# Two groups of an MLP go together block by block, and the indexer's first half moves into the MLP's tail

## The chip, the cores and the metric

The kernel runs on one core of a Trainium2 chip. The metric is the device time of one execution in microseconds (us), as the median of repeated runs. A profile is one further execution, seen by the hardware profiler.

The engines are named as in the profile: PE is the matrix engine, DVE the vector engine, ACT the scalar engine, POOL the GpSimd engine, and SP the engine that issues most DMA transfers. SBUF is the on-chip memory, PSUM the accumulators that PE writes.

## The reference

Four residual layers on 512 tokens of width 1024, in single precision: a mixer of stick-breaking attention and a state-space model, an MLP, a mixer of sparse attention ("DSA"), an MLP. Each is followed by a layer norm.

```python
x = layer_norm(ALPHA * x + h, ln_mix_g[i], ln_mix_b[i])
x = layer_norm(ALPHA * x + sq_relu_mlp(x, mlp_w1[i], mlp_w2[i]), ln_ffn_g[i], ln_ffn_b[i])

def sq_relu_mlp(x, w1, w2):
    return jnp.square(jax.nn.relu(x @ w1)) @ w2          # D_FF = 4096
```

The sparse attention lets a small "indexer" choose for each query the 128 keys that it attends to:

```python
# mixer_dsa: qi has 8 heads of 32, ki one head of 32, wi 8 weights
rel = jax.nn.relu(jnp.einsum('bqhd,bsd->bqsh', qi_b, ki))
score = jnp.einsum('bqsh,bqh->bqs', rel, wi_b) * idx_scale
score = jnp.where(causal, score, -jnp.inf)
_, idx = lax.top_k(score, topk)                          # topk = 128
```

The first 128 queries (block 0) have at most 128 keys, so nothing is chosen for them.

## The kernel before, in words

Tokens are cut in four blocks of 128. The residual stream `x` is in SBUF with tokens on partitions; its transpose is kept as two halves, `xhi` and `xlo`, whose sum is the single-precision value, and a product is made of three matmuls (hi by hi, hi by lo, lo by hi: `mm3` at L129, and L380 to L382). Weights come raw by DMA (L101); ACT rounds them to `whi` (L104), and DVE or POOL subtracts to get `wlo` (L105).

The order of instructions on each engine is not written by hand. A scheduler under the kernel's language orders each engine's queue when the program is built, from the order in which the code asks for the operations and from its own estimate of when each is ready. The queue is then fixed: an instruction that waits holds up all that stand behind it on its engine.

**The first MLP** (`mlp`, L205). Hidden units are cut in eight groups of 512. Groups 0 to 5 go through three passes with fewer products (`down_chunk`). Groups 6 and 7 are done plainly: `up_split` gives their hidden units as halves, and `mlp_block` (L371) multiplies one block of 128 tokens by 512 output columns in PSUM and adds that to `x` (L387). Before the change, the first half of the columns of group 6 is done for all four blocks. Then, block by block, `both` does group 7's first half of the columns and groups 6 and 7 together in the second half, with the norm of a block (`layer_norm`, L172) following the blocks. A norm is a chain over DVE (L181 to L183), POOL (L184), DVE (L185, L189), eight PE transposes (L199), and a split by ACT (L202) and DVE (L203) into `xhi` and `xlo`. Its parameters `gb` are loaded at L168.

**The indexer** (`index_scores`, L1009) belongs to the next mixer. For two halves of the tokens, c=0 (tokens 0 to 255) and c=1 (256 to 511), it projects key and weights (64 columns of weights, `psi`) and twice 128 query columns (72 matmuls), splits the results into halves (`split`, L854 and L855), writes them to DRAM (`kd`, `qd`) and reads them back in another layout (`kist`, `qist`; L1053 to L1062). `score_block` (L1070) then does a query block: eight matmuls (`psx`, L1078), eight relus on ACT (L1080) and eight weighted sums on DVE (L1081). Blocks 1, 2 and 3 have 256, 384 and 512 keys. `top_keys` (L1106) finds the 128 best of each query on DVE: 16 steps of a MAX (eight maxima, L1113) and a MATCH_REPLACE (L1114), for block 1 first and then for blocks 2 and 3 in turn. `dist` (L1119) marks the keys that were chosen, and the attention (`sparse_attention`, L1121) needs it at L1143, the first step behind its logits (`psl`, L1136).

Besides, the mixer projects V (L1101 to L1103), K and Q (`psa`, L131 to L133), which fill PE while DVE works on the top-k.

Of the kernel before, what the change touches and what calls it, by code (L numbers as in the profile page):

```python
# [11 lines left out]
ALU = mybir.AluOpType  # L12
# [23 lines left out]
class Trunk:  # L36
# [59 lines left out]
    def weights(self, srcs, n=1024, eng=None, pool=None, parts=1, tag=None):  # L96

        nc = self.nc
        raw, hi, lo = self.w_tiles(pool, tag)
# [8 lines left out]
    def w_cols(self, w, c0, eng=None, pool=None, tag=None):  # L108
# [4 lines left out]
        hi, lo = self.weights(srcs, eng=eng, pool=pool, tag=tag)  # L113
        return hi.rearrange("p (k c) -> p k c", c=P), lo.rearrange("p (k c) -> p k c", c=P)
# [90 lines left out]
    def mlp(self, w1, w2, g, b, last):  # L205
# [7 lines left out]
        with self.tc.tile_pool(name=self.nm("mlp"), bufs=2, side="right", reuse_waits="tile") as hp:  # L213
# [17 lines left out]
            def up_split(grp):  # L231
                hhi, hlo = h_tile(F32R), h_tile(F32R)
                for f in range(4):
                    ps = self.proj_fm(w1, grp * 512 + f * P, None)
                    h = hp.tile([P, S], F32, tag="r", bufs=1, name=self.nm("r"))
# [5 lines left out]

            for hs in up_raw(0, True):
                pass
            u = hp.tile([P, 2, 512], F32, tag="u", bufs=1, name=self.nm("u"))
# [8 lines left out]
            ng = 8  # L253
            for grp, h in ((6, got[3]), (7, got[7])):
                ws = [[self.w_rows(w2, grp * 512 + i * 256, half * 512, pool=hp if half or grp < ng - 1 else self.wp,
                                   tag=(("b12", "b11")[half] if grp < ng - 1 else "b21") if half or grp < ng - 1
                                   else None)
                       for i in range(2)] for half in range(2)]
                part = lambda half, h=h, ws=ws: (*h, ws[half])
                if grp == ng - 2:  # L260
                    for t in range(NB):
                        self.mlp_block([part(0)], t, 0, False)
                    held = part(1)
                else:
                    def both(t):
                        self.mlp_block([part(0)], t, 0, False)
                        n = 256 if last and t == NB - 1 else 512
                        for c0 in range(0, 512, n):
                            self.mlp_block([held, part(1)], t, 1, False, c0, n)
                    self.blocks_and_norms([lambda t=t: both(t) for t in range(NB)], self.ln_params(g, b), last,  # L270
                                          2 if last else 1)
# [683 lines left out]
    def mixer_dsa(self, w_in, w_out, g, b):  # L955
        nc, tc = self.nc, self.tc
        act, vec, pool = nc.scalar, nc.vector, nc.gpsimd
        with tc.tile_pool(name="m1", bufs=1, reuse_waits="tile") as mp, \
                tc.tile_pool(name="m1d", bufs=1, space=DRAM) as dp, \
# [6 lines left out]
            for h in range(16):  # L966
                pool.memset(sc[64 * (h % 2):64 * (h % 2) + 64, h // 2:h // 2 + 1], -0.125 / slope(h))
            with tc.tile_pool(name="idxs", bufs=1, side="right", reuse_waits="tile") as sp:
                accs, drm = self.index_scores(w_in, ip, sp, dp)
# [39 lines left out]
    def index_scores(self, w_in, op, ip, dp):  # L1009
# [3 lines left out]
        drm = op.tile([P, S], F32, name="drm")  # L1013
        cm = op.tile([P, S], F32, name="cm")
# [3 lines left out]
        pool.memset(cm, 0.0)  # L1018
        pool.affine_select(out=cm, in_=cm, pattern=[[-1, S]], compare_op=ALU.is_ge, fill=LOW,
                           base=S - P, channel_multiplier=1)  # L1020


        raw, hi, lo = self.w_tiles()
# [8 lines left out]
        wk = [t[:, 0:n].rearrange("p (k c) -> p k c", c=64) for t in (hi, lo)]  # L1032
        wts = [wk] + [self.w_cols(w_in, 1536 + i * P) for i in range(2)]
        wi = op.tile([P, NB, 8], F32, name="wi")

# [166 lines left out]
```

## Time and profile before

| | |
|---|---|
| median of 3 runs | 1167.16 us (1166.71 to 1168.52) |
| the profiled execution | 1165.24 us |
| its span, first to last instruction | 1163.5 us |
| granted PE clock over the span | 0.988 |
| busy: PE, DVE, ACT, POOL | 1108.7, 841.5, 532.4, 173.1 us |

Times in the views are microseconds from the start of the span. A timeline row has start, duration, engine, line, operation, `out<-in`, shape and count; in brackets stands the idle time ahead of it and what ended it. A row of waits has engine, what was waited with, `<-` what it waited for, total, times, longest. A row of the windows has a stretch, its length, the busy time of PE, PE's weight loads, DVE, ACT and POOL with their numbers of instructions, then the granted PE clock (1.00 is full), the share of time in which DMA was busy, and GB/s. A row of the chain has start, duration and what the end waited on. A group's row ends with the total, the mean in ns and the idle time ahead of it. Matmuls overlap: their duration is longer than their spacing, and costs here go by the spacing.

### The profile page before, as it was taken

To read this page: it belongs to the slowest core of one execution; us is meant where nothing else is said; L and a number is where in the kernel's file an instruction comes from. 1 tells how busy PE (TensorE), PEld (TensorE's weight loads), DVE (VectorE), ACT (ScalarE), POOL (GpSimd) and SP (SyncE) were. 2 spreads that over 40 slices of the span, in tenths; PEclk is the share of its full clock that TensorE was granted. 3 is DMA by queue.
4 is the path that set the end of the run, shared out by engine and by line. 5 is a ranking of instruction groups with operands and counts; after the bars stand their busy time and mean duration, and the time that the engine had idled before them with its cause. 6 is when DMAs were issued, how large, how long until landed. Compare 5 with 4: busy or idle time off the path is not lost.

```text
span 1163.5 us, 15569 instructions
## 1 busy us (share of the span) xinstructions
PE 1108.7 (95%) x5860; PEld 923.6 (79%) x5860; DVE 841.5 (72%) x1255; ACT 532.4 (46%) x832; POOL 173.1 (15%) x201
## 2 busy tenths in 40 slices
PE   7988998999999999999999959998999999999997
PEld 6877876788888888888888847776988888888886
DVE  7997598694666866975668997538548668587736
ACT  5534387324444544554135427642445445445510
POOL 1043230320000000000021744325000000000001
PEclk9999999999999999999999989999999999999999
DMA  7526683751242242333056850025304414415101
GB/s 244 142 64 156 188 220 100 211 151 37 72 145 91 75 150 66 110 108 79 1 141 160 217 164 1 19 69 186 109 19 127 129 35 145 127 38 162 37 1 73
DMA packets 147307, 126.99 MB, mean 109 GB/s; under 512 B 24353, under 2 KB 115297, under 8 KB 147233
## 3 DMA queue, kind: packets, MB, share of 16 engines
q1 hardware_dynamic: 145552, 123.59, 36.7%
q10 hardware_dynamic: 1680, 2.41, 0.6%
q8 instruction: 46, 0.75, 0.3%
q14 instruction: 29, 0.23, 0.1%
HBM read 105.80 MB, written 5.37 MB: 96 GB/s over the span
## 4 chain that ended last, share of the span: by engine, by line
PE 80%; DVE 12%; DMA 3%; issue 2%; ACT 2%; SPq 1%; POOLq 0%; DVEq 0%; ACTq 0%
PE psa L133 11%; PE psa L132 11%; PE psa L131 11%; PE psb L313 7%; PE psb L311 7%; PE psb L312 7%; PE pso L949 3%; PE psb L382 3%; PE psb L381 3%; PE psb L380 2%; PE pst L942 2%; DVE acc L1114 2%; DVE top L1113 2%; PE psb L841 2%; PE psb L842 2%
## 5 line engine op out<-in xcount | busy, mean ns | idle before, releaser
L133 PE MATMUL psa<-xhi,wlo 128*128 128x512 f32 (+1 forms) x720 | 267.1, 372 | 0.0
L132 PE MATMUL psa<-xlo,whi 128*128 128x512 f32 (+1 forms) x720 | 266.6, 371 | 0.0
L131 PE MATMUL psa<-xhi,whi 128*128 128x512 f32 (+1 forms) x720 | 265.6, 371 | 0.2 <-ACT xhi L202 0.2
L104 ACT CAST whi<-raw 128x1024 fp32r<-128x1024 f32 (+1 forms) x129 | 133.3, 1046 | 200.9 <-PE psa L132 130.1
L105 DVE TENSOR_TENSOR wlo<-raw,whi 128x1024 fp32r<-128x1024 f32 (+1 forms) x102 | 127.8, 1258 | 80.5 <-ACT whi L104 79.7
L132 PEld LDWEIGHTS psa<-xlo,whi 128*128 128x128 f32 x720 | 135.7, 188 | 23.4 <-DVE xlo L203 0.4
L133 PEld LDWEIGHTS psa<-xhi,wlo 128*128 128x128 f32 x720 | 135.8, 189 | 23.1
L131 PEld LDWEIGHTS psa<-xhi,whi 128*128 128x128 f32 x720 | 135.0, 188 | 23.1 <-ACT xhi L202 0.5
L299 DVE TENSOR_TENSOR wlo<-b,whi 128x1024 fp32r<-128x1024 f32 x84 | 102.5, 1221 | 43.0 <-ACT whi L298 42.8
L311 PE MATMUL psb<-whi,whi 128*128 128x512 f32 x336 | 130.7, 389 | 0.0
L312 PE MATMUL psb<-wlo,whi 128*128 128x512 f32 x336 | 130.7, 389 | 0.0
L313 PE MATMUL psb<-whi,wlo 128*128 128x512 f32 x336 | 129.7, 389 | 0.0
L298 ACT CAST whi<-b 128x1024 fp32r<-128x1024 f32 x84 | 88.3, 1051 | 42.0 <-PE psb L313 30.2
L105 POOL TENSOR_TENSOR wlo<-raw,whi 128x1024 fp32r<-128x1024 f32 x27 | 70.8, 2632 | 132.5 <-ACT whi L104 131.4
L184 POOL TENSOR_TENSOR rs<-rs,two 128x1 f32<-128x1 f32 x16 | 22.7, 1417 | 423.8 <-DVE rs L183 423.8
L312 PEld LDWEIGHTS psb<-wlo,whi 128*128 128x128 f32 x336 | 63.1, 188 | 13.2
L313 PEld LDWEIGHTS psb<-whi,wlo 128*128 128x128 f32 x336 | 63.1, 188 | 13.1
L311 PEld LDWEIGHTS psb<-whi,whi 128*128 128x128 f32 x336 | 63.1, 188 | 13.0
L293 DVE TENSOR_TENSOR b<-b,b 128x1024 f32<-128x1024 f32 x48 | 63.1, 1320 | 11.4 <-DMA b<-in_w_dram 10.9
L298 ACT CAST whi<-h 128x1024 fp32r<-128x1024 f32 x36 | 38.0, 1054 | 54.0 <-PE psb L312 34.0
L299 DVE TENSOR_TENSOR wlo<-h,whi 128x1024 fp32r<-128x1024 f32 x36 | 43.9, 1220 | 14.0 <-ACT whi L298 13.5
L841 PE MATMUL psb<-whi,xhi 128*128 128x512 f32 x128 | 51.5, 410 | 0.8 <-DVE x L848 0.6
(263 smaller groups left out, 1955.4 us busy)
## 6 DMA issues: line engine op xcount, KB each, us to landing
raw<-in_w_dram SPq DMA_DIRECT2D x80, 512.0 KB, 4.1
b<-in_w_dram SPq DMA_DIRECT2D x48, 512.0 KB, 4.5
raw<-in_w_in_dram SPq DMA_DIRECT2D x29, 512.0 KB, 4.5
raw<-in_w_out_dram SPq DMA_DIRECT2D x16, 512.0 KB, 4.8
qst<-hl SPq DMA_DIRECT2D x48, 128.0 KB, 3.5
kst<-hl SPq DMA_DIRECT2D x24, 256.0 KB, 4.7
gb<-in_ln_g_dram SPq DMA_DIRECT2D x4, 512.0 KB, 4.1
gb<-in_ln_b_dram SPq DMA_DIRECT2D x4, 512.0 KB, 5.0
```

Source lines behind the costliest of these rows:

```text
L104: nc.scalar.copy(hi[:, c], raw[:, c])
L105: (eng or nc.vector).tensor_tensor(lo[:, c], raw[:, c], hi[:, c].bitcast(F32), ALU.subtract)
L131: mm(ps, lhi, rhi, start=start, stop=False)
L132: mm(ps, lhi, rlo, start=False, stop=False)
L133: mm(ps, llo, rhi, start=False, stop=stop)
L293: vec.tensor_tensor(o, p, q, op)
L298: act.copy(hi, src)
L299: vec.tensor_tensor(lo, src, hi.bitcast(F32), ALU.subtract)
L311: mm(ps, lh, bhi[:, k, :], start=i + k == 0, stop=False)
L312: mm(ps, lh, blo[:, k, :], start=False, stop=False)
L313: mm(ps, ll, bhi[:, k, :], start=False, stop=i + k == 2)
L841: nc.tensor.matmul(ps, chi[:, k, tok], whi, start=i == 0, stop=False)
```

## The change

- In the first MLP, groups 6 and 7 are multiplied together for both halves of the columns: 24 matmuls in one accumulation, twice per block. The pass of group 6 alone is gone there, and with it four of the twelve evacuations. The second MLP keeps it.
- The order of the tail is written out: blocks 0 and 1, norm 0, block 2, norm 1, the first part of the indexer, block 3, norm 2, norm 3, the second part of the indexer.
- The indexer's first part is c=0: keys and weights of tokens 0 to 255, the queries of tokens 128 to 255 alone (block 0 needs none; 128 columns per matmul in place of 256), the way through DRAM, and the scores of block 1. The second part is c=1, up to the way through DRAM; its scores and all top-k steps stay in the mixer.
- The buffers that this needs (`drm`, `kist`, `wi`, `acc1`) live from before the first MLP, the weight and split buffers of the indexer lie in the MLP's pools, the buffers `u` and `r` of the MLP share the tile of the norm's parameters, and the causal mask `cm` becomes a DVE operation at the start of each score block.

```diff
-            u = hp.tile([P, 2, 512], F32, tag="u", bufs=1, name=self.nm("u"))
+            ur = self.cp.tile([P, 2, D], F32, tag="gb", bufs=1, name=self.nm("ur"))
+            u, r = (ur[:, i, :].rearrange("p (h c) -> p h c", c=512) for i in range(2))
...
-            for grp, h in ((6, got[3]), (7, got[7])):
...
+            parts = lambda half: [(*got[3], w6[half]), (*got[7], w7[half])]
+            if last:
+                for t in range(NB):
+                    self.mlp_block([(*got[3], w6[0])], t, 0, False)
...
+            def both(t):
+                self.mlp_block(parts(0)[last:], t, 0, False)
+                n = 256 if last and t == NB - 1 else 512
+                for c0 in range(0, 512, n):
+                    self.mlp_block(parts(1), t, 1, False, c0, n)
+            gb = self.ln_params(g, b)
...
+                both(0)
+                both(1)
+                norm(0)
+                both(2)
+                norm(1)
+                e = early(hp)
+                next(e)
+                both(3)
+                norm(2)
+                norm(3)
+                next(e)
...
+            hls = hp.tile([P, 2, 2, 256], F32R, tag="b11", bufs=2, name=self.nm("hls"))
...
+                n = P if i and c == 0 else 256
+                at = slice(tok.stop - n, tok.stop)
...
-                hl = self.hl_tile()[:, :, 0:256]
+                hl = hls[:, i % 2, :, 0:n]
...
+            if c == 0:
+                qst = hp.tile([P, 1024], F32R, tag="b11", bufs=2, name="qist1")[0:96].rearrange(
+                    "p (h t) -> p h t", t=P)
+                self.load_index_queries(qst, P)
+                slots = itertools.count()
+                self.score_block(1, qst, self.acc1, lambda: rel[:, next(slots) % 4, :])
+            yield
...
-            nc.vector.scalar_tensor_tensor(acc, r, wi[:, qb, h:h + 1], acc if h else cm[:, S - nk:],
-                                           ALU.mult, ALU.add)
+        nc.vector.tensor_scalar(acc, self.drm[:, S - nk:], BIG, LOW, ALU.is_ge, ALU.mult)
+            nc.vector.scalar_tensor_tensor(acc, r, self.wi[:, qb, h:h + 1], acc, ALU.mult, ALU.add)
```

How this moves the queues, at three places. A number behind a name is that of the tile or weight. In the changed kernel the lines of `mlp_block` are L392 to L394 and L399, `psx` is L1114, the score sums are L1117, the splits of the indexer L867, and MAX and MATCH_REPLACE L1147 and L1148.

PE before, from the last matmul of the first MLP (L382, block 3) to the first of c=1 (`psi_5119`); `pst` are the transposes of norms 2 and 3:

```order
L382 MATMUL psb_4878<-whi_4688,h_4359 128x512
L131 MATMUL psi_5019<-xhi,whi_4995 64x256
...
L199 MATMUL pst_4914<-ident,x 128x128 x4
...
L131 MATMUL psi_5050<-xhi,whi_5003 128x256
...
L131 MATMUL psi_5079<-xhi,whi_5009 128x256
...
L199 MATMUL pst_4938<-ident,x 128x128 x4
...
L1065 MATMUL psw_5113<-ident,wiT_5048 128x8 x2
L131 MATMUL psi_5119<-xhi,whi_4995 64x256
```

PE in the changed kernel, from the end of norm 1's transposes to the first of c=1 (`psi_5105`); block 3 is `psb_5001` and `psb_5027`:

```order
L199 MATMUL pst_4838<-ident,x 128x128 x3
L131 MATMUL psi_4873<-xhi,wx_4850 64x256 [waits Activation_49]
...
L133 MATMUL psi_4930<-xhi,wx_4865 128x128
...
L392 MATMUL psb_5001<-whi_4591,h_4034 128x512
...
L1114 MATMUL psx_4969<-kist,qist_4964 128x256 [waits DMAHW6_49,DMAHW5_49,DMAHW7_49,DMAHW3_49,DMAHW2_49]
...
L393 MATMUL psb_5027<-wlo_4628,h_4363 128x512
...
L199 MATMUL pst_5063<-ident,x 128x128 x4
...
L1114 MATMUL psx_4985<-kist,qist_4964 128x256 [waits Activation_49]
...
L199 MATMUL pst_5087<-ident,x 128x128 [waits DVE_49]
...
L131 MATMUL psi_5105<-xhi,wx_4850 64x256 [waits Activation_49]
```

The 72 matmuls of c=0 went from behind block 3 to ahead of it, and four `psx` of block 1, which wait for DRAM, stand ahead of its last eight matmuls. Between block 3 and c=1 only the transposes of norms 2 and 3 and four `psx` are left.

DVE before, from the evacuation of block 3 (L387 with `psb_4878`) to the end of its norm (L189):

```order
L387 TENSOR_TENSOR x<-x,psb_4878 128x512
L181 BN_STATS st_4928<-x 128x6
L182 BN_AGGR mv_4929<-st_4928 128x2
L183 TENSOR_SCALAR rs_4930<-mv_4929 128x1
L185 SCALAR_TENSOR_TENSOR x<-x,mv_4929,gb_4693 128x1024
L203 TENSOR_TENSOR xlo<-pst_4914,xhi 128x4x128
L203 TENSOR_TENSOR xlo<-pst_4921,xhi 128x4x128
L189 SCALAR_TENSOR_TENSOR x<-x,rs_4930,gb_4693 128x1024
```

DVE in the changed kernel, the same stretch (L399 with `psb_5027`):

```order
L399 TENSOR_TENSOR x<-x,psb_5027 128x512
L1117 SCALAR_TENSOR_TENSOR acc_2456<-rel_4872,wi,acc_2456 128x256
L105 TENSOR_TENSOR wlo_5484<-raw_5482,whi_5483 128x1024
L181 BN_STATS st_5077<-x 128x6
L105 TENSOR_TENSOR wlo_5524<-raw_5522,whi_5523 128x1024
L203 TENSOR_TENSOR xlo<-pst_5063,xhi 128x4x128
...
L182 BN_AGGR mv_5078<-st_5077 128x2
...
L183 TENSOR_SCALAR rs_5079<-mv_5078 128x1
L185 SCALAR_TENSOR_TENSOR x<-x,mv_5078,gb_4638 128x1024
L1117 SCALAR_TENSOR_TENSOR acc_2456<-rel_4872,wi,acc_2456 128x256
L189 SCALAR_TENSOR_TENSOR x<-x,rs_5079,gb_4638 128x1024
```

Two weight splits and four score sums of block 1 came in between (two of the sums are at the places left out).

DVE before, from the last split of c=1 (`psi_5179`) to the first sum of block 2 (`acc_5258`):

```order
L855 TENSOR_TENSOR hl_5204<-psi_5179,hl_5204 128x256
L1081 SCALAR_TENSOR_TENSOR acc_5217<-rel_5225,wi,acc_5217 128x256
...
L1113 MAX top_5342<-acc_5217 128x8
L1114 MATCH_REPLACE acc_5217<-top_5342,acc_5217 128x256
...
L1113 MAX top_5357<-acc_5217 128x8
L1081 SCALAR_TENSOR_TENSOR acc_5258<-rel_5261,wi,cm 128x384
```

DVE in the changed kernel, the same stretch (`psi_5162` to `acc_5223`):

```order
L867 TENSOR_TENSOR hls_5103<-psi_5162,hls_5103 128x256
L1111 TENSOR_SCALAR acc_5223<-drm 128x384
...
L1147 MAX top_5316<-acc_2456 128x8
L1148 MATCH_REPLACE acc_2456<-top_5316,acc_2456 128x256
...
L1147 MAX top_5331<-acc_2456 128x8
L1117 SCALAR_TENSOR_TENSOR acc_5223<-rel_5235,wi,acc_5223 128x384
```

The sums of block 1 left this stretch. The top-k steps of block 1 (`acc_2456` is `acc1`) stand where they stood: behind the last split of c=1, five and a half of them ahead of the first sum of block 2.

More of the change, by code (lines that the diff above doesn't have):

```diff
@@ L94, in w_tiles, with weights @@
                 wp.tile([P, 1024], F32R, tag="wlo", bufs=4, name=self.nm("wlo")))
-    def weights(self, srcs, n=1024, eng=None, pool=None, parts=1, tag=None):
+    def weights(self, srcs, n=1024, eng=None, pool=None, parts=1, tag=None, tiles=None):
         nc = self.nc
-        raw, hi, lo = self.w_tiles(pool, tag)
+        raw, hi, lo = tiles or self.w_tiles(pool, tag)
         for view, src in srcs(raw):
@@ L234, in up_split @@
                     ps = self.proj_fm(w1, grp * 512 + f * P, None)
-                    h = hp.tile([P, S], F32, tag="r", bufs=1, name=self.nm("r"))
+                    h = r[:, f % 2, :]
                     nc.scalar.activation(h, ps, AF.Relu)
@@ L252, in mlp @@
                 hs = got[-1]
-            ng = 8
-            for grp, h in ((6, got[3]), (7, got[7])):
[L255 to L271, printed above, removed]
+            rows = lambda grp, half, **kw: [self.w_rows(w2, grp * 512 + i * 256, half * 512, **kw) for i in range(2)]
@@ new lines, in mlp @@
+            w6 = [rows(6, half, pool=hp, tag=("b12", "b11")[half]) for half in range(2)]
+            parts = lambda half: [(*got[3], w6[half]), (*got[7], w7[half])]
+            if last:
+                for t in range(NB):
+                    self.mlp_block([(*got[3], w6[0])], t, 0, False)
+            w7 = [rows(7, half, **(dict(pool=hp, tag="b21") if half and last else {})) for half in range(2)]
+            def both(t):
[3 more added lines that the diff above has]
+                    self.mlp_block(parts(1), t, 1, False, c0, n)
@@ new lines, in mlp @@
+            gb = self.ln_params(g, b)
+            if last:
+                self.blocks_and_norms([lambda t=t: both(t) for t in range(NB)], gb, last)
+            else:
+                norm = lambda t: self.layer_norm(t, gb, last)
+                both(0)
[9 more added lines that the diff above has]
+                next(e)
@@ L967, in mixer_dsa @@
                 pool.memset(sc[64 * (h % 2):64 * (h % 2) + 64, h // 2:h // 2 + 1], -0.125 / slope(h))
+            accs = [None, self.acc1] + [ip.tile([P, S], F32, tag="acc", bufs=2, name=self.nm("acc"))[:, :(qb + 1) * P]
+                                        for qb in (2, 3)]
+            drm = self.drm
             with tc.tile_pool(name="idxs", bufs=1, side="right", reuse_waits="tile") as sp:
-                accs, drm = self.index_scores(w_in, ip, sp, dp)
+                qst = sp.tile([96, 8, 256], F32R, name="qist")
+                self.load_index_queries(qst, 256)
+                for qb in (2, 3):
+                    rel = lambda: sp.tile([P, S], F32, tag="rel", bufs=4, name=self.nm("rel"))
+                    self.score_block(qb, qst[:, :, (qb - 2) * P:(qb - 1) * P], accs[qb], rel)
             vec.tensor_copy(dist[:, 0, 0:P], drm[:, S - P:])
@@ L1017, in index_scores, with tiles @@
                            base=S - P, channel_multiplier=1)
[L1018 to L1023, printed above, removed]
+        def tiles(tag):
+            raw = self.wp.tile([P, 1024], F32, tag="raw", bufs=3, name=self.nm("raw"))
+            return raw, *(hp.tile([P, 1024], F32R, tag=tag, bufs=2, name=self.nm("wx")) for _ in range(2))
+        raw, hi, lo = tiles("b21")
         n = KT * 64
@@ L1053, in index_scores @@
                     nc.sync.dma_start(kd.rearrange("a d t -> d a t"), hl[rows].bitcast(F32))
[L1054 removed]
+                    wiT = rel[0:8, 3, :]
                     act.activation(wiT, ps[0:8], AF.Copy, scale=0.0625)
                 else:
[L1057 to L1062 removed]
+                    nc.sync.dma_start(self.qd[:, (i - 1) * P:i * P, 0:n].rearrange("a d t -> d a t"),
+                                      hl.bitcast(F32))
+            nc.sync.dma_start(self.kist[0:64, tok].bitcast(F32), kd.rearrange("a d t -> (a d) t"))
+            nc.sync.dma_start(self.kist[64:96, tok].bitcast(F32), kd[0])
             ps = self.psb.tile([P, 2, 8], F32, tag="psb", name=self.nm("psw"))
```

64 lines of the change are left out of this document (30 added, 34 removed).

## The prediction

> **What bounds the kernel now.** I read the page's busy shares first, then the chain of waits around the end of the first MLP, then each engine's timeline there. PE is busy for 95% of the span, so the first question is whether this change touches a stretch that PE sets. The chain (start, us, what) says that from the last MLP matmul to the attention it is not PE:
>
> ```profile
> 606.97 4.92 DMA kd<-hl
> 611.91 0.38 ACT hl L854
> 613.58 4.65 DMA qd<-hl
> 619.11 4.51 DMA qist<-qd
> 623.86 0.94 PE psx L1078 x4
> 639.18 2.56 DVE acc L1081
> 646.08 2.54 DVE acc L1081
> 650.34 0.47 DVE top L1113
> 650.81 2.51 DVE dist L1119
> ```
>
> After the index projections of tokens 256 to 511 the work goes through DRAM (kd, qd, qist), then the scores (psx on PE, acc on DVE), then from 650.3 the top-k of query blocks 2 and 3, which is DVE alone. PE fills this time with the V, K and Q projections, runs out, and waits:
>
> ```profile
> PE psl L1136 <- DVE pst L1143: 14.6, 1, 14.6
> 697.74 0.55 DVE L1143 CUSTOM_DVE_ANT_0 pw<-psl,dist 128x384 f32<-128x384 f32 x1
> 698.35 3.92 PE L1136 MATMUL psl<-kst,qst 128*128 128x384 f32 x16 [14.62 <-DVE pst L1143]
> ```
>
> So 14.6 us of PE work can leave or enter this stretch for nothing, while every us by which DVE ends the top-k later or earlier (697.7) moves the attention, the second MLP and the end. The forecast is that one shift. Ahead of it, up to 600, PE does set the pace (20.00 busy of 20.00):
>
> ```profile
> 560.00:580.00 20.00, 20.00 (x94) 16.65 (x93) 11.62 (x18) 1.07 (x2) 2.91 (x2) 1.00 0.00 1
> 589.21 0.39 PE L382 MATMUL psb<-whi,h 128*128 128x512 f32 x1
> 589.44 0.28 PE L131 MATMUL psi<-xhi,whi 128*64 128x256 f32 x1
> 593.07 0.28 PE L131 MATMUL psi<-xhi,whi 128*128 128x256 f32 x1
> 597.74 1.04 PE L199 MATMUL pst<-ident,x 128*128 128x128 f32 x8
> 600.00 0.45 PE L131 MATMUL psi<-xhi,whi 128*64 128x256 f32 x2
> 608.42 0.28 PE L133 MATMUL psi<-xhi,wlo 128*128 128x256 f32 x1
> ```
>
> The MLP's last matmul is at 589.2. The index projections of tokens 0 to 255 (c=0) follow at once and lie under the evacuation and norm of block 3, whose transposes come at 597.7; those of tokens 256 to 511 (c=1) run from 600.0 to 608.5. From 589.4 to 600 PE is never idle.
>
> **The change part by part.** The top-k of blocks 2 and 3 ends at: last MLP matmul + norm of block 3 + c=1 projections + DRAM + scores + 47 us of steps. I cost after minus before on this path.
>
> (a) The combination. All 48 matmuls per block remain; twelve of them move from a pass of their own into a block's run. Four evacuations go (DVE L387, 0.69 each), which lay beside PE's full stretch and save nothing there. The u and r buffers now share the parameters' tile, so the load of gb waits for the last relu of group 7:
>
> ```profile
> gb<-in_ln_g_dram SPq DMA_DIRECT2D x4, 512.0 KB, 4.1
> ```
>
> Two blocks of 48 matmuls at 0.227 (589.44 − 589.21), 21.8 us, lie between that relu and the first use of gb: 0. For block 0 the last quarter of group 7 is needed 21 x 0.227 = 4.8 us after its projection ends, with a relu, a square, a weight cast and two splits on ACT and DVE in between. I take 0, with a bound of 1.2: each of the five as long as the 1.22-us split at 605.27 below makes 6.1.
>
> (b) c=0 now stands ahead of the last MLP block, on the path of PE. 24 matmuls of 64 columns take 0.113 each ((590.81 − 589.44) / 12), 48 have 128 columns in place of 256. A 256-column matmul takes 0.12 (39 of them between 593.07 and 597.74); eight 128-column transposes take 0.79 from their start to the next start, 0.10 each:
>
> ```profile
> 590.81 1.03 PE L199 MATMUL pst<-ident,x 128*128 128x128 f32 x8
> 591.60 0.36 PE L131 MATMUL psi<-xhi,whi 128*64 128x256 f32 x1
> ```
>
> So halving the columns saves little: 24 x 0.113 + 48 x 0.11 = +8.0; bounds 5.6 (half of 0.12) and 8.5 (all of it). Before, this work was free, under the norm of block 3.
>
> (c) The first of these matmuls waits for the split of the norm of block 1: +1.2 (ACT xhi and DVE xlo below), and four of the score matmuls stand ahead of the last eight MLP matmuls, 4 x 0.12: +0.5. Bounds together 0.5 and 2.9.
>
> (d) PE then waits in its queue, eight MLP matmuls short of the end, for block 1's queries to return from DRAM. The rows (SP issues) give the way:
>
> ```profile
> 602.07 0.37 SPq L1057 DMA_DIRECT2D qd<-hl  x1
> 604.41 1.31 SPq L1061 DMA_DIRECT2D qist<-qd  x3
> 618.24 1.31 SPq L1061 DMA_DIRECT2D qist<-qd  x3
> ```
>
> Split 0.8 (two of 0.4, as hl at 611.91 and 612.3), write 2.3 (602.07 to 604.41, quiet queues) or 4.65 (qd at 613.58, with weight loads in flight), reads 5.4 (618.24 to 623.62): 8.5 to 10.9, and the cover is 40 x 0.227 = 9.1. Behind this wait stand the last eight MLP matmuls, and block 3's evacuation and norm wait for them. +0.7; bounds 0 and 5 (two loads ahead of it on SP, as for kd at 606.97).
>
> (e) The norm of block 3. DVE's rows before, with ACT's cast beside it and the group of the sums of block 1:
>
> ```profile
> 589.64 0.69 DVE L387 TENSOR_TENSOR x<-x,psb 128x512 f32<-128x512 f32 x1 [0.46 <-PE psb L382]
> 592.60 1.28 DVE L203 TENSOR_TENSOR xlo<-pst,xhi 128x512 fp32r<-128x512 f32 x2
> 593.79 1.28 DVE L189 SCALAR_TENSOR_TENSOR x<-x,rs,gb 128x1024 f32<-128x1024 f32 x1
> 605.27 1.22 DVE L105 TENSOR_TENSOR wlo<-raw,whi 128x1024 fp32r<-128x1024 f32 x1 [3.88 <-ACT whi L104]
> 617.21 0.43 DVE L1113 MAX8 top<-acc 128x8 f32<-128x256 f32 x1
> 618.19 0.43 DVE L1113 MAX8 top<-acc 128x8 f32<-128x256 f32 x1
> L1081 DVE SCALAR_TENSOR_TENSOR acc<-rel,wi,acc 128x256 f32<-128x256 f32 x7 | 3.4, 483 | 1.1 <-ACT rel L1080 0.7
> 598.38 1.07 ACT L202 CAST xhi<-pst 128x512 fp32r<-128x512 f32 x2 [1.65 <-PE pst L199]
> ```
>
> From evacuation to the end of L189 took 5.4 us (589.64 to 595.0), and the transposes then stood until 597.7 behind c=0. In the new order the same DVE stretch also holds two weight splits (2 x 1.2) and four score sums (4 x 0.5): 5.4 + 2.4 + 2.0 = 9.8, and the transposes go at once, with 1.6 to 2.3 more to the first c=1 matmul as from 597.7 to 600.0: 11.4 to 12.1 after the evacuation starts at +0.2, against 10.6 before. +0.8; bounds 0 and +2. Nothing covers it now, so PE is idle for some 6 us.
>
> (f) What PE does after such an idle stretch is in the windows; the granted clock is the fourth number from the end:
>
> ```profile
> 805.00:811.00 6.00, 1.17 (x6) 0.75 (x5) 6.00 (x12) 0.00 (x0) 2.06 (x2) 0.96 0.02 5
> 811.00:815.00 4.00, 4.00 (x16) 3.40 (x15) 4.00 (x7) 1.66 (x3) 1.75 (x2) 0.64 0.02 4
> 698.30:702.00 3.70, 3.65 (x16) 3.56 (x16) 3.70 (x16) 3.66 (x12) 1.01 (x2) 0.60 0.00 0
> ```
>
> Both follow a PE idle time (most of 805 to 811, and the 14.6 above). 4 us at 0.64 lose 1.4 us, and c=1 is 8.5 us of matmuls that DVE waits for: +1.5, bounds 0 and 1.7. The Trainium skill, "TensorE: Matmul & The Clock Gate", Part 1, states the rule: after an idle window of about 3.4 us the array runs at half clock until about 3.4 us of activity. By it the loss would be 1.7; it speaks against this change, and the two windows agree with it.
>
> (g) What is gained. Before, the last c=1 split was held until kd had landed (611.89), since it reuses that buffer; its matmuls were done at 608.5 + 0.3. After, the kd write has no weight load ahead of it in the queue: −2.8, bounds −3.1 and −1.5. The qd write then takes 2.3 rather than 4.65: −2.4, bounds 0 and −2.9.
>
> (h) Scores of block 1 leave DVE's queue behind c=1: eight sums of 0.5, 4 us. That pays only if DVE is the later one there. It isn't: in the new order the same 5.5 top-k steps (0.97 each, 617.21 on) still stand between the last split and the first sum of block 2, and that sum waits for qist. They fill 5.4 of the 9.6 us of DRAM. So 0. From then on DVE's work is as before with one more weight split (+1.2), less what changes in its holds: sums that start while POOL splits weights last 2.4 to 2.6 us in place of 0.6 to 0.8:
>
> ```profile
> 632.33 2.42 POOL L105 TENSOR_TENSOR wlo<-raw,whi 128x1024 fp32r<-128x1024 f32 x1 [36.79 <-ACT whi L104]
> 632.81 2.35 DVE L1081 SCALAR_TENSOR_TENSOR acc<-rel,wi,acc 128x384 f32<-128x384 f32 x1
> 631.90 0.60 DVE L1081 SCALAR_TENSOR_TENSOR acc<-rel,wi,acc 128x384 f32<-128x384 f32 x1
> ```
>
> Four such holds (632.81, and 639.18, 646.08 and 650.81 in the chain) cost about 7.4 us. I expect three or four again: +0.2, bounds −7 and +1.2.
>
> Sum: 8.0 + 1.7 + 0.7 + 0.8 + 1.5 − 2.8 − 2.4 + 0.2 = +7.7. PE's stall before the attention grows to some 30 us, which costs nothing further. The profiled execution took 1165.24, so its like should take 1172.9; the median of the runs shown is 1.92 above that execution: 1174.8. The gains rest on what the queues do, and the bounds of (b) and (h) reach further down than up, so I name 1174.0.
>
> **The rivals.** 0.2% is 2.3 us, about what a measurement of this kernel can tell from no change; faster and slower mean beyond that.
>
> Faster: POOL's splits leave the scores. The new order loads four K and Q weights ahead of c=1's kd, POOL's first one among them, where before one stood there; if POOL runs ahead by the 9.6 us that DVE waits for DRAM, the four holds of 7.4 us go from the path. It decides the sign once the rest of the sum is below +5, as it is with (b) and (c) at their lower bounds: 7.7 − 2.4 − 1.2 − 7.4 = −3.3, 1163.9. Against it: each of those splits waits for ACT's cast, which the new order puts behind block 2's scores. Chance 0.10.
>
> No change: the holds shrink by half (−3.7) and the norm of block 3 does not lengthen or slow the clock (−2.3): +1.7, 1168.9. For it: the gains of (g) may be larger, as every DRAM row here was contended. Chance 0.13.
>
> Slower still: the wait in (d) decides. If the write goes behind the loads of gb and weights, 5 us in place of 0.7 with eight MLP matmuls behind it, the sum is +12.0, 1179.2; with every other term at its upper bound (+0.5, +1.2, +1.2, +0.2, +1.3, +0.9, +1.0) it is 1185.5. It decides from a return later than 9.1 us after the last c=0 matmul. Chance 0.12.
>
> The forecast, +4 to +12, 1171 to 1179: 0.65. Range 1166 to 1181: it leaves out the first rival, a little of the second and the upper half of the third. Faster 0.10, same 0.13, slower 0.77.
>
> **What would show it.** Right: c=0 matmuls (psi) ahead of the last MLP block at 0.1 each; a PE idle time of 5 to 9 us between that block and c=1, and a clock of about 0.6 behind it; the last split of c=1 not held by kd; the first top-k step of blocks 2 and 3 about 8 us later than 650.3, and PE's wait for the softmax's minimum (14.6 before) at about 30 us. Wrong: that step no later than 652 (then (b) was hidden or (h) paid), or the wait at the block-1 scores longer than 3 us (then (d) was too small).

## The result and the profile after

| | before | after |
|---|---|---|
| median | 1167.27 us (1166.71 to 1168.52, 4 runs) | 1180.19 us (1179.85 to 1181.19, 4 runs) |
| the profiled execution, its span | 1165.24, 1163.5 us | 1180.32, 1178.5 us |
| ratio | | 1.0111, 95% interval 1.0093 to 1.0128 |

The change costs 12.9 us by the medians, 15.1 by the two profiled executions. The forecast was slower by 6.8 to 7.7, so the sign is right and the size is half. The profiled execution of the kernel before is 2.0 us below the median of its runs, that of the changed kernel 0.1 above.

The place of the missing half is seen when the span is cut at the marks of the prediction. First, PE's timeline of the changed kernel, in the lines that answer to those of the kernel before (last up-projection, first c=0 matmul, last MLP matmul, transposes of norm 3, first of c=1, attention):

```profile
548.35 0.40 PE L133 MATMUL psa<-xhi,wlo 128*128 128x512 f32 x1
583.93 0.50 PE L131 MATMUL psi<-xhi,wx 128*64 128x256 f32 x3 [0.24 <-ACT xhi L202]
584.91 0.33 PE L132 MATMUL psi<-xlo,wx 128*64 128x256 f32 x1 [0.48 <-DVE xlo L203]
...
602.31 0.64 PE L1114 MATMUL psx<-kist,qist 96*128 96x256 f32 x4
...
604.42 0.39 PE L394 MATMUL psb<-whi,h 128*128 128x512 f32 x1
...
614.02 1.97 PE L199 MATMUL pst<-ident,x 128*128 128x128 f32 x8 [7.85 <-DVE x L189]
615.81 0.91 PE L131 MATMUL psi<-xhi,wx 128*64 128x256 f32 x3
...
708.99 3.35 PE L1170 MATMUL psl<-kst,qst 128*128 128x384 f32 x10 [10.57 <-DVE pst L1177]
```

The reader is to see the idle times in brackets. c=0 now stands ahead of the last MLP block and waits 0.24 and 0.48 us for the halves of norm 1; the eight matmuls behind the scores of block 1 (602.31) wait for nothing; PE is idle for 7.85 us ahead of the last transposes; and the wait before the attention is 10.57 us, not the 30 of the prediction.

Second, DVE's timeline, with the last split, the first weighted sum of blocks 2 and 3, the first top-k step on block 2's 384 keys (650.25 before) and the start of the attention's first step behind its logits (`pw`):

```profile
626.02 0.42 DVE L867 TENSOR_TENSOR hls<-psi,hls 128x256 fp32r<-128x256 f32 x1 [2.35 <-ACT hls L866]
637.17 0.62 DVE L1117 SCALAR_TENSOR_TENSOR acc<-rel,wi,acc 128x384 f32<-128x384 f32 x1 [4.72 <-ACT rel L1116]
662.43 0.55 DVE L1147 MAX8 top<-acc 128x8 f32<-128x384 f32 x1
662.90 1.05 DVE L1153 TENSOR_TENSOR dist<-acc,drm 128x256 f32<-128x256 f32 x1
708.38 0.55 DVE L1177 CUSTOM_DVE_ANT_0 pw<-psl,dist 128x384 f32<-128x384 f32 x1
```

The same marks of the kernel before: last up-projection and last split in these rows, the others in the prediction.

```profile
543.88 0.39 PE L133 MATMUL psa<-xhi,wlo 128*128 128x512 f32 x1
612.32 0.42 DVE L855 TENSOR_TENSOR hl<-psi,hl 128x256 fp32r<-128x256 f32 x1 [0.84 <-ACT hl L854]
650.25 0.55 DVE L1113 MAX8 top<-acc 128x8 f32<-128x384 f32 x1
```

The marks are the ends of the last up-projection, of the last MLP matmul and of the last split, and the starts of the first matmul of c=1, of the first `psx` of block 2 (623.86 and 636.20, in the chains), of that top-k step and of that `pw`. The length of each stretch, from mark to mark:

| stretch, us | before | after | difference | forecast |
|---|---|---|---|---|
| start to the last up-projection | 544.3 | 548.8 | +4.5 | 0 |
| to the last MLP matmul | 45.3 | 56.1 | +10.7 | +10.4 (a to d) |
| to the first matmul of c=1 | 10.4 | 11.0 | +0.6 | +0.8 (e) |
| to the end of the last split of c=1 | 12.7 | 10.6 | −2.1 | −1.3 (f, kd of g) |
| to the scores of block 2 | 11.1 | 9.8 | −1.4 | −2.4 (qd of g) |
| to the top-k of blocks 2 and 3 | 26.4 | 26.2 | −0.2 | +0.2 (h) |
| to the attention | 47.5 | 46.0 | −1.5 | 0 |
| to the end of the span | 465.7 | 470.2 | +4.4 | 0 |

The six stretches that the change edits sum to +6.2 before rounding, near the +7.7 of the prediction. The other 8.9 us lie where the change is not meant to act: up to the end of the first MLP's up-projections, and from the attention to the end of the second MLP.

What differs there is the matmuls themselves. Of the costliest groups of the page, this is one of the three of the products in both MLPs' first six hidden groups, before and after (total, then mean ns of one):

```profile
L311 PE MATMUL psb<-whi,whi 128*128 128x512 f32 x336 | 130.7, 389 | 0.0
```

```profile
L323 PE MATMUL psb<-whi,whi 128*128 128x512 f32 x336 | 132.6, 395 | 0.0
```

The same instructions, in the same number, take 6 ns more each. The windows show what that does to the pace: of one stretch that PE fills and where the granted clock is 1.00, before and after.

```profile
300.00:350.00 50.00, 50.00 (x222) 41.42 (x221) 39.55 (x41) 27.36 (x33) 0.00 (x0) 1.00 0.39 120
```

```profile
300.00:350.00 50.00, 50.00 (x219) 40.76 (x218) 38.03 (x38) 26.11 (x31) 0.00 (x0) 1.00 0.38 115
```

222 matmuls in 50 us, then 219. From the starts of all matmuls of the first MLP in the timeline, the products stand 0.2267 us apart before and 0.2329 after, the up-projections of 512 columns 0.2267 and 0.2272. So the 504 products of an MLP lose 504 x 0.0062 = 3.1 us, and its 672 up-projections 0.4: 3.5 per MLP. The last two groups of the first MLP, which stand in the tail, lose some 0.7 more. Of the +4.5 and +4.4 measured, 1.2 each lies ahead of an MLP: its first up-projection starts at 253.2 in place of 252.0, and in the second MLP 123.2 in place of 122.0 behind the start of the attention. These 1.2 us have no cause shown; two executions of one kernel differ by as much.

### The profile page after: what moved, and what is told of

Its sections match the earlier page's. It is cut to its first block, busy times and chain, and to the rows that moved or that the text cites. A ratio compares the mean times of both kernels' runs of the same rounds, so it can differ in the third digit from the quotient of the medians.

```text
span 1178.5 us, 15538 instructions
## 1 busy us (share of the span) xinstructions
PE 1121.6 (95%) x5860; PEld 927.3 (79%) x5860; DVE 837.7 (71%) x1254; ACT 531.6 (45%) x832; POOL 170.7 (14%) x199
## 4 chain that ended last, share of the span: by engine, by line
PE 80%; DVE 13%; DMA 3%; issue 2%; ACT 1%; SPq 1%; POOL 0%; POOLq 0%; DVEq 0%; ACTq 0%
PE psa L132 11%; PE psa L133 11%; PE psa L131 11%; PE psb L325 7%; PE psb L323 7%; PE psb L324 7%; PE pso L961 3%; PE psb L392 3%; PE psb L394 3%; PE psb L393 3%; PE pst L954 2%; DVE acc L1148 2%; DVE top L1147 2%; PE psl L1170 2%; PE psb L853 2%
## 5 line engine op out<-in xcount | busy, mean ns | idle before, releaser
L324 PEld LDWEIGHTS psb<-wlo,whi 128*128 128x128 f32 x336 | 63.1, 188 | 15.1
L325 PEld LDWEIGHTS psb<-whi,wlo 128*128 128x128 f32 x336 | 63.1, 188 | 15.1
L323 PEld LDWEIGHTS psb<-whi,whi 128*128 128x128 f32 x336 | 63.1, 188 | 14.7
L202 ACT CAST xhi<-pst 128x512 fp32r<-128x512 f32 x24 | 13.3, 588 | 88.1 <-PE pst L199 88.0
```

Of the source, the lines that this page charges most:

```text
L323: mm(ps, lh, bhi[:, k, :], start=i + k == 0, stop=False)
L324: mm(ps, lh, blo[:, k, :], start=False, stop=False)
L325: mm(ps, ll, bhi[:, k, :], start=False, stop=i + k == 2)
```

## The experiments

Where tiles lie in SBUF is known from the built program. The change adds buffers that live from before the first MLP (`drm`, `kist`, `wi`, `acc1`: 5248 bytes per partition) and takes `u` and `r` (6144) out of the pool of the MLP, which so shifts by 896 bytes. All of these but `wi`, with 128 bytes, are multiples of 256. Start of a tile, in bytes modulo 256, for the two operands that a product reads:

| | weights' pool (stationary operand of the products) | MLP's pool (moving operand) |
|---|---|---|
| before | 224 | 224 |
| after | 224 | 96 |

My theory was then: the tail costs what the prediction says, and a product is slower when its two operands start at different places modulo 256. Rivals were that the moving operand's own place counts, that it counts modulo 512, or that something else in the new order slows PE.

**1 and 2: padding of 128 bytes, added to the changed kernel, and to the kernel before.** No instruction changes in either.

```diff
         self.acc1 = ip.tile([P, 256], F32, name="acc1")
+        ip.tile([P, 32], F32, name="pad")
```

```diff
-        self.mlp(a["w1"][0], a["w2"][0], g[1:2], b[1:2], False)
+        with self.tc.tile_pool(name=self.nm("pad"), bufs=1, side="right") as pp:
+            pp.tile([P, 32], F32, name=self.nm("pad"))
+            self.mlp(a["w1"][0], a["w2"][0], g[1:2], b[1:2], False)
```

> The changed kernel with one unused tile of 128 bytes per partition beside the indexer's persistent tiles; no instruction differs, only the place of the MLP's tiles in SBUF: their moving operands (whi and wlo of the b blocks) then start at 224 modulo 256 bytes, like the stationary halves (224), where the changed kernel has them at 96 and the kernel before at 224. Theory of placement: the product's matmuls (L323 to L325) go at 0.227 us instead of 0.233, as before the change; with 504 of them in each MLP that is 3.2 us twice, and the matmuls of the tail and of psa add about 1: 1180.2 - 7.5 = 1172.7. Rival (the 4.5 us lost ahead of the tail come from the shared u and r buffers or from the order of the queues): no change, 1180. Rival (the phase counts modulo 512, where moving is at 224 and stationary at 480): no change, 1180.

> The kernel before, with an unused tile of 128 bytes per partition held during each MLP, which puts the moving operands of the products at 96 modulo 256 bytes while the stationary ones stay at 224. No instruction differs. Theory of placement: spacing 0.233 in place of 0.227, 3.2 us per MLP and a little for psb of the tail: 1167.3 + 7 = 1174. Rival (the slower matmuls belong to what the change does): 1167.

Measured, 4 runs each: the changed kernel with the padding takes 1172.37 us (1171.87 to 1173.01) against 1166.58 for the kernel before, ratio 1.0048 (1.0030 to 1.0066). The kernel before with the padding takes 1174.09 (1173.37 to 1175.19), ratio 1.0063 (1.0047 to 1.0079). The groups of PE's lines between 300 and 540 us, of the padded changed kernel, and of the padded kernel before:

```profile
L131 PE MATMUL psa<-xhi,whi 128*128 128x512 f32 x185 | 72.0, 389 | 0.0
L323 PE MATMUL psb<-whi,whi 128*128 128x512 f32 x168 | 65.4, 389 | 0.0
```

```profile
L131 PE MATMUL psa<-xhi,whi 128*128 128x512 f32 x180 | 70.1, 390 | 0.0
L311 PE MATMUL psb<-whi,whi 128*128 128x512 f32 x168 | 66.3, 395 | 0.0
```

The 6 ns go from the one and come to the other. So the new order is not needed for the loss, which is 7.8 us in the changed kernel (1180.19 less 1172.37) and 7.5 in the kernel before. The span of the padded changed kernel is 1170.5, 7.0 more than before; cut at the same marks it has +0.9, +10.0, +0.6, −2.2, −1.1, −0.2, −1.5 and +0.6. The six in the middle, +5.5, are what the edits of the order cost; the first and the last, +1.5, lie ahead of the two MLPs and are the part without a cause shown.

**3 and 4: 64 bytes, and 384.** The pads are `[P, 16]` in the kernel before and `[P, 96]` in the changed one.

> The same with 64 bytes: moving operands at 160 modulo 256 (32 modulo 128), stationary at 224 (96 modulo 128). If any mismatch of phase counts: spacing 0.233 or more. If only the half of a 256-byte line counts in which the row starts (160 and 224 are in the same half): 0.227.

> The changed kernel with an unused tile of 384 bytes: moving operands at 480 modulo 512 like the stationary ones. If the phase counts modulo 512, this one has 0.227 and the one with 128 bytes 0.233; if modulo 256, both have 0.227 and about 1172.7.

Measured, one run each: 1173.70 and 1173.18. With 64 bytes (operands at 160 and 224) the products stand 0.2333 us apart, as slow as with 128; with 384 they stand 0.2267 apart. In the changed kernel 128 and 384 bytes of padding both bring the operands to one place modulo 256, but only 384 brings them to one place modulo 512, and both are fast. So a difference of 64 costs as much as one of 128, and one of 256 costs nothing.

**12: 128 bytes at the head of the weights' pool.** This tells the relation of the two operands from the place of either. It moves the stationary operand of the products to 96 as well, where the moving one of the changed kernel lies, and with it all weights of that pool away from `xhi` and `xlo`, which stay at 224.

```diff
         self.wp = ctx.enter_context(tc.tile_pool(name="w", bufs=1))
+        self.wp.tile([P, 32], F32, name="pad")
```

> The changed kernel without the padding of the index's pool, but with 128 bytes of padding at the head of the weights' pool: the stationary halves of the MLP's products and all weights of that pool start at 96 of 256 bytes in place of 224; the products' moving operands stay at 96, and the moving xhi and xlo of the up-projections stay at 224. If what counts is that the two operands of a matmul start at the same place modulo 256: the products (L324 to L326) go back to a mean spacing of 0.2267 us from 0.2329, and the up-projections (psa, some 2000 matmuls over the kernel) go from 0.2270 to 0.233, time 1180 - 6 + 12 = 1186 (1181 to 1191). If the moving operand's own place counts: products stay at 0.233, up-projections at 0.227, time 1180. If the stationary operand's own place counts (224 good): both at 0.233, time 1192.

Measured: 1180.64, one run. PE's groups between 300 and 540 us of this kernel:

```profile
L132 PE MATMUL psa<-xhi,whi 128*128 128x512 f32 x180 | 71.0, 395 | 0.0
L324 PE MATMUL psb<-whi,whi 128*128 128x512 f32 x168 | 65.5, 390 | 0.0
```

The two kinds have changed places: products 390 ns and 0.2274 apart, up-projections 395 and 0.2330. So it is the relation of the two operands that counts, as expected. The time I expected, 1186, was too high: I had counted some 2000 up-projections, those of the mixers among them. By the spacings of the two traces the 672 of an MLP lose 3.9 us and its products win back 2.8, +1.1 per MLP; measured is +0.5 in all, in one run, and the runs of the kernel before beside it differ by up to 5.7.

**5: c=0 behind the last MLP block again,** in the padded kernel, by the order written out. This tests term (b).

```diff
                 e = early(hp)
-                next(e)
                 both(3)
+                next(e)
                 norm(2)
```

> The changed kernel with the 128-byte tile, and with the first part of the indexer asked for behind block 3 in place of ahead of it: the 72 matmuls of c=0 lie under the norm of block 3 again, the joint blocks and all else stay. Theory by the prediction's terms: (b) and (c) go, -8.0 and -1.7; the idle time of PE in the norm of block 3 and its half clock go, -2.0; against that the scores of block 1 wait for DRAM in the middle of c=1's matmuls, 0 to 5. 1172.4 - 11.7 + 3 = 1164, between 1161 and 1168. Rival (the tail's loss comes from joining the groups or from the new buffers, not from where c=0 stands): no change, 1172.

Measured: 1169.15 (1167.55 to 1170.65, 10 runs), ratio 1.0012 (0.9998 to 1.0027). A miss: 3.2 us better than the padded kernel by the medians (on another chip) where I expected 8. The last MLP matmul is back at 45.3 us behind the last up-projection, 10.0 earlier, but the last split of c=1 comes only 1.5 earlier. PE's waits between 540 and 740 show where the gain went, and a row of the windows what followed:

```profile
PE psl L1171 <- DVE pst L1178: 11.8, 1, 11.8
PE psx L1115 <- DMA qd<-hls: 2.2, 1, 2.2
PE psw L1092 <- ACT rel L1084: 1.3, 1, 1.3
PE psx L1115 <- DMA qist<-qd: 1.2, 1, 1.2
```

```profile
611.00:613.00 2.00, 2.00 (x10) 2.00 (x10) 1.69 (x4) 1.49 (x5) 0.00 (x0) 0.50 0.00 0
```

The scores of block 1 now stand in the middle of c=1's matmuls, ahead of the last 24, and wait in PE's queue for DRAM (2.2, on `qd`): the wait of term (d), without the MLP block that covered it. The eight of them take 2.2 more, the granted clock behind the wait is 0.50, and the last split waits 0.75 for `kd`, whose keys now come last.

**8: the scores of block 1 behind c=1 as well,** on top of 5.

```diff
+            else:
                 slots = itertools.count()
                 self.score_block(1, qst, self.acc1, lambda: rel[:, next(slots) % 4, :])
```

> As e5_pad_c0_late, with the scores of block 1 asked for behind the projections of c=1, as in the kernel before. What is left of the change is the joint groups, the shared buffers, the 128-column queries and the other split buffers. Theory: in e5_pad_c0_late the loss moved from block 3 to the middle of c=1, where eight score matmuls wait 2.2 us for DRAM and take 2.4 themselves, and the norms' transposes and the keys of c=1 come late behind them; with that gone it is as the kernel before or up to 3 us faster (the last split no longer waits for kd): 1165 to 1167.5. Rival (joining the groups costs by itself): 1169 or more.

Measured: 1165.68 (1164.11 to 1167.07, 10 runs), ratio 0.9994 (0.9984 to 1.0003): the time before. From the last up-projection to the end of the last split it has 66.0 us (68.5 before), to the attention 152.8 (153.5). What is left of the change in it, the two groups block by block, the shared buffers and the longer lives, costs nothing that these runs can tell. So the 5.8 us of the padded kernel come from c=0 and the scores of block 1 standing ahead of block 3 and c=1.

**6 and 7: the 16 top-k steps of block 1 ahead of c=1's splits,** in the padded kernel (6) and with c=0 late as in 5 (7). The prediction says that the early scores pay only if DVE has something to do with them.

```diff
             tok = slice(c * 256, c * 256 + 256)
+            if c:
+                for step in range(TOPK // 8):
+                    vec.max(self.top1, self.acc1)
+                    vec.match_replace(self.acc1, self.top1, self.acc1, MARK)
...
-        for step in range(TOPK // 8):
+        for step in range(0 if qbs == (1,) else TOPK // 8):
```

> The changed kernel with the 128-byte tile, and with the 16 top-k steps of block 1 asked for between the norm of block 3 and the second part of the indexer, so that they stand on DVE ahead of c=1's splits and under the way through DRAM. Theory (h): the early scores cost without a return only because these steps still stand behind c=1; moved up, 10.5 of them, 0.97 each, leave the stretch between the first sum of block 2 and the top-k of blocks 2 and 3, and 4.7 us of DVE's wait for DRAM are filled: -10, less what PE's order of the scores then holds back, and at most the 10.6 us that PE had in hand before the attention. 1172.4 - 8 = 1164. Rival (that stretch is set by POOL's holds and PE's order of psx and not by DVE's work): no change, 1172.

> Both of the other two. The scores of block 1 then come about 8 us later against c=1, and only some five of the steps go ahead of the first sum of block 2, as in the kernel before. Theory: nearly no gain from the early steps, as e5_pad_c0_late or 1 to 2 us less, 1163. Rival (gains add): 1172.4 - 8 - 8 = 1156.

Measured: 1166.99 (ratio 0.9996, 0.9982 to 1.0011) and 1167.16 (0.9996, 0.9984 to 1.0008), 10 runs each. Both are 3 to 4 us above what I expected, yet 6 is 5.4 below the padded kernel by the medians (on another chip). The top-k of blocks 2 and 3 then starts 16.5 us earlier (96.5 in place of 113.0 behind the last up-projection), but the attention only 4.0. The wait of PE ahead of the attention in 6 says what took over:

```profile
PE psl L1176 <- DMA qst<-hl: 5.9, 1, 5.9
```

Not DVE but the queries of the attention (`qst`), which DMA moves from one place in SBUF to another, come last now. The gain of DVE past that is covered.

**9 and 11: PE kept busy ahead of the last transposes,** by 26 unread matmuls in the padded kernel, asked for behind the last MLP block (9) or behind norm 2 (11). This tests term (f).

```diff
                 both(3)
+                warm = self.psb.tile([P, 512], F32, tag="psb", name="warm")
+                for _ in range(26):
+                    nc.tensor.matmul(warm, got[3][0][:, 0, 0:P], got[3][0][:, 0, :], start=True, stop=True)
                 norm(2)
```

> Set aside by its successor below: 26 more matmuls of 512 columns, whose result nobody reads, on PE between block 3 and the transposes of both norms 2 and 3; the order puts norm 2's transposes behind them. Clock theory (f): the transposes of norm 3 take 1.0 instead of 2.0 and the first 3 us of c=1 run at full clock: -2.0, but norm 2's split may come later: 1170 to 1172.4. Rival (the half clock does not reach DVE's path): 1172.4.

> The changed kernel with 128 bytes of padding (1172.37) plus 26 unread matmuls of 512 columns on PE, this time asked for behind norm 2, so that DVE keeps its order and only PE's idle time ahead of the last norm's transposes is filled. If that idle time costs by the clock behind it alone, as my term (f) says: granted clock 1.00 in place of 0.50 at the transposes, transposes 1.0 in place of 1.97 us, c=1's matmuls 1 us shorter, time 1170.4 (1169.8 to 1171.3). If the 3.6 us of the kernel with the matmuls behind the last block came from DVE's other order: 1172 and unchanged spacing between the last evacuation and the last split. If both halves matter: about 1170.4 here and 1168.8 there.

Measured: 1168.80 (1166.21 to 1170.03, 12 runs), ratio 1.0014 (1.0005 to 1.0023), and 1170.24 (1168.46 to 1173.33, 12 runs), 1.0028 (1.0016 to 1.0040): 3.6 and 2.1 below the padded kernel by the medians, on other chips. That kernel's ratio is 1.0048 (1.0030 to 1.0066), so only 9 is clear of it; 9 is also below what I expected. The second number is the one I expected of the clock, and it is not the clock. The windows of 11:

```profile
609.00:611.00 2.00, 0.07 (x1) 0.07 (x2) 1.96 (x4) 0.00 (x0) 1.59 (x13) 1.00 0.00 0
611.00:612.00 1.00, 1.00 (x8) 0.79 (x8) 0.27 (x1) 0.38 (x1) 0.40 (x5) 0.87 0.16 29
612.00:613.00 1.00, 0.92 (x5) 0.62 (x4) 0.76 (x2) 0.79 (x2) 0.00 (x0) 0.50 0.58 205
613.00:614.00 1.00, 1.00 (x6) 1.00 (x6) 0.53 (x1) 0.00 (x0) 0.00 (x0) 0.50 0.73 233
614.00:615.00 1.00, 1.00 (x7) 1.00 (x6) 0.00 (x0) 0.00 (x0) 0.00 (x0) 0.50 1.04 414
615.00:616.00 1.00, 1.00 (x10) 1.00 (x8) 0.00 (x0) 0.00 (x0) 0.00 (x0) 0.93 0.42 168
```

1.93 us without work were left, and the clock fell to 0.50 all the same, though only some 0.8 us after work had begun again at 610.93. From the last MLP matmul to the end of the last split 11 takes 21.5 us, as the padded kernel without the extra matmuls. Its gain lies behind that, in the write of the queries to DRAM. SP's rows of the changed kernel, of 11, and of 6:

```profile
624.31 0.58 SPq L1085 DMA_DIRECT2D qd<-hls  x1
624.94 0.46 SPq L1088 DMA_DIRECT2D kist<-kd  x1
626.47 0.37 SPq L1085 DMA_DIRECT2D qd<-hls  x1
630.67 1.31 SPq L1104 DMA_DIRECT2D qist<-qd  x3
```

```profile
620.46 0.38 SPq L1089 DMA_DIRECT2D qd<-hls  x1
620.89 0.47 SPq L1091 DMA_DIRECT2D kist<-kd  x1
623.26 0.37 SPq L1089 DMA_DIRECT2D qd<-hls  x1
625.46 1.30 SPq L1108 DMA_DIRECT2D qist<-qd  x3
```

```profile
621.70 0.38 SPq L1091 DMA_DIRECT2D qd<-hls  x1
624.39 0.37 SPq L1091 DMA_DIRECT2D qd<-hls  x1
628.63 1.31 SPq L1110 DMA_DIRECT2D qist<-qd  x3
```

From the issue of the last write of queries to the read that needs it 4.20 us pass in the changed kernel (4.32 with the padding) and 2.20 in 11. The order on SP does not make the difference. 6 has the order of 11, with the first write ahead of the reads of `kist`, and takes 4.24; 4 and 12 have the order of the changed kernel and take 2.64. What the slow ones share is a load of instructions by DMA. The changed kernel's windows from the write's issue on, and the row of the DMA queues for 628.30 to 629.45:

```profile
626.47:628.27 1.80, 1.80 (x17) 1.80 (x16) 1.73 (x7) 0.00 (x0) 0.00 (x0) 1.00 0.43 145
628.27:629.45 1.18, 1.18 (x12) 1.18 (x11) 1.11 (x4) 0.37 (x1) 0.00 (x0) 1.00 0.07 15
```

```profile
q8 instruction: 1, 0.02, 6.2%
```

The write is all but done at 628.3. Then one packet of 16 KB with instructions runs alone, from 628.33 to 629.46, and the write's last two packets start at 629.45 and 629.57. In the padded kernel and in 6, four and sixteen packets of the write follow such a load in the same way. In 5, 9 and 11 (2.2 to 2.3 us) no load falls into the write, and in 4 and 12 one starts just as the write's last packet ends. So these 2 us of 11 depend on where a load of instructions falls in the one execution that was profiled, and not on PE. Where it falls in the other runs is not known.

In 9 the clock does stay at 1.00, and what that brings is seen in three rows of its PE:

```profile
607.69 1.09 PE L199 MATMUL pst<-ident,x 128*128 128x128 f32 x8 [0.22 <-DVE x L189]
609.02 0.65 PE L131 MATMUL psi<-xhi,wx 128*64 128x256 f32 x3 [0.24 <-ACT xhi L202]
610.28 0.33 PE L132 MATMUL psi<-xlo,wx 128*64 128x256 f32 x1 [0.61 <-DVE xlo L203]
```

The transposes take 1.09 in place of 1.97, but c=1 then waits 0.24 and 0.61 for the halves of the norm. From the first transpose to the end of the last split: 11.9 us, and 12.3 without. So the full clock brings 0.4 us net here. But the 0.61 is a wait for DVE, which has another order in 9: it does the xlo half of norm 2 behind norm 3, and has no idle time there. With the old order the clock may be worth up to 1.0, and no run has both. The other gains of 9 are a write of the queries without a load of instructions, as in 11 (2.2 us from write to read), and again DVE's order: from the evacuation of block 3 to the end of L189 it takes 7.4 in place of 9.1.

**10: 6 and 11 together.**

> As e6_pad_top1_early, with 26 more matmuls of 512 columns whose result nobody reads, on PE between the transposes of norm 2 and those of norm 3 (5.9 us in an idle time of 7.9). Clock theory (f): transposes of norm 3 at 1.0 us instead of 2.0, c=1 at full clock, granted clock 1.00 in the stretch behind them: the last split of c=1 comes 2.0 earlier, and 1167.0 - 2 = 1165. Rival (what follows is set by PE's and DMA's own work, as PE's last wait there was for Q from DMA): 1167.

Measured: 1165.99 (1164.04 to 1169.34, 10 runs), ratio 0.9996 (0.9985 to 1.0007). The clock did not stay at 1.00 here: 1.94 us without work were left ahead of the transposes, and it is 0.50 from 610 to 613. So 10 does not test the clock either. Kernels 8 and 10 have the lowest medians, and neither differs measurably from the kernel before; no version here beats it.

## Why the prediction was right and wrong

- **The missing half: no term for the MLPs' own matmuls.** The prediction says that ahead of 600 "PE does set the pace" and that "the forecast is that one shift", and costs (a), the shared and longer-lived buffers, at 0 by their waits alone. That is the step that failed. The new buffers move the MLP's pool by 128 bytes modulo 256, and each product of both MLPs takes 0.2329 us in place of 0.2267. It is worth 7.8 us (1180.19 less 1172.37), shown by 1, 2 and 12. The prediction counted the instructions of PE and did not ask whether one of them still lasts as long. That 1180.19 still lies in the range of 1166 to 1181 is luck: the range reached so far up for the wait of (d), which was 0.
- **(a) to (d), +10.4:** 10.0 with the padding, from these parts: c=0's 72 matmuls take 8.3 without the wait among them, for the 8.0 of (b); the waits of (c) are 0.72 for 1.2; four `psx` take 0.5, and two small transposes `psw`, which moved along and which the prediction left out, 0.2; the wait of (d) is 0 for 0.7, as block 1's queries were back when PE came to their scores at 602.31. Some 0.3 is left unassigned. It is not (a): in 8, which keeps (a), the stretch to the last MLP matmul is 45.3 us as before.
- **(e), +0.8:** +0.6. The chain from evacuation to L189 takes 9.1 (604.85 to 613.96), for 9.8 forecast, and PE's idle time 7.85 for "some 6".
- **(f), +1.5:** the clock fell as said, to 0.50, and the transposes took 1.97 for 1.04, but 9 puts the net cost at 0.4, at most some 1.0. So (f) was too large.
- **(g), −2.8 and −2.4:** the last split was not held, and came at once, as said. The write of the queries still took 4.06 us in the chain of waits of the changed kernel, for 4.65, though no weight load was in flight: its last packets came behind a load of instructions. Where none falls into the write it takes the 2.3 forecast (2.20 to the read in 9 and 11). Another 0.9 came since SP issues the write at once behind the split (626.44 to 626.47; before, 612.7 to 613.58). −1.4 in all.

```profile
612.68 1.29 DVE x L189
614.02 1.97 PE pst L199 x8
...
626.47 4.06 DMA qd<-hls
631.52 4.42 DMA qist<-qd
636.20 0.94 PE psx L1114 x4
```

- **(h), +0.2:** −0.2, and then −1.5 on to the attention, most of it one hold less (`dist` 1.05 us in place of 2.59). That the early scores of block 1 are worth nothing without the top-k steps is borne out by 6: with the steps moved too, the loss of the tail can no longer be measured.
- **PE's stall at 30 us:** 10.6. The prediction does not work the 30 out; with PE as early as before and DVE 7.7 later it would be 22. But PE's filler, the V, K and Q projections, stands behind c=1, and came later itself: PE arrives at 698.4 (708.99 less 10.57), 14.7 us later than before (698.35 less 14.62), and DVE ends only 10.6 later.
- **The rivals:** the holds of POOL shrank (2.07, 1.45, 1.79 and 1.05 us for 2.35, 2.56, 2.54 and 2.59) but did not vanish, and the stretch that they stand in got only 0.2 shorter; the wait in (d) did not decide; and the padded kernel, which has the forecast's mechanism alone, is slower by 5.8 us. What took the time above the forecast was none of the three: they all concerned the order in the tail.

## What to carry to other kernels

A change can slow matmuls that it does not touch, if it shifts where their operands lie: when PE sets the pace, compare one matmul's mean duration or spacing before and after, in a stretch that the change doesn't touch, ahead of any story on the order. Work moved ahead on the engine that sets the pace is paid in full there, and is paid back only if the work that it releases is moved as well. And when a stall is filled, look what waited behind it unseen: here the halves of a norm and the transfer of the attention's queries. One profiled execution can also hold something that belongs to none of the edits, as the load of instructions in the write of the queries.

## What was not expected of the hardware

- A matmul of 512 columns in this precision takes 0.2267 us when its moving and its stationary operand start at the same place modulo 256 bytes, and 0.2329 to 0.2333 when they differ by 64 or 128, at a granted clock of 1.00 in both. It is the relation that counts: with both at 96 (0.2274) it is nearly as fast as with both at 224. Which part of the chip makes it is not shown, nor whether other shapes or types have it.
- PE's clock fell to half behind an idle time of 1.93 us (11), of 1.94 (10) and of 2.2 (5). The Trainium skill, "TensorE: Matmul & The Clock Gate", Part 1, has the clock fall after an idle window of about 3.4 us, and rise after as much activity. The second half agrees (0.50 from 612 to 615 and 0.93 in the next us in 11); the first does not, as here much less idle time was enough, in 11 behind 5 us of matmuls without a gap.
- A load of 16 KB of instructions by DMA took 1.1 us (628.33 to 629.46 in the changed kernel), and the last two packets of a 256 KB write came behind it: 4.20 us from write to read, for 2.20 in 11, where no load falls into the write. That both use the same DMA engine would explain it and is not shown.
